# One channel-major step more ahead of the second column group's seven-product steps, in two eighths of a two-layer MLP

## The chip, the cores and the metric

The kernel runs on one core of a Trainium2 chip. The metric is the device time of one execution in microseconds (us). TensorE (PE) multiplies matrices, its weight loads are listed as PEld; VectorE (DVE), ScalarE (ACT) and GpSimd (POOL) work on tiles; SyncE (SP), ACT and POOL issue DMA transfers. Each engine takes its instructions in the order of the program and waits on semaphores for the others.

## What is computed

A decoder trunk of two layers on x of 256 positions by 2048 channels, all in float32. The change lies in the MLP, the second half of each layer:

```
h2 = rms_norm(x, norm2_g[l])
x = x + jnp.square(jax.nn.relu(h2 @ w_up[l])) @ w_down[l]
```

`w_up` is 2048 x 8192 and `w_down` 8192 x 2048. Ahead of the MLP a layer has one input projection, eight attention heads, eight gated channel groups and an output projection; after both layers comes a last norm.

## The kernel before

**Three products for one.** Every float32 weight tile of 128 x 1024 is loaded by SP into `raw` (7 buffers, L155), rounded by ACT into a high part `hi` (6 buffers, L167) and subtracted by DVE into a low part `lo` (6 buffers, L177). The moving operand stands in two parts as well. A product is then three matmuls: high by high (L400), low weight by high (L402), high weight by low (L404).

**The MLP in eighths.** The hidden 8192 channels are worked in eighths of 1024. In the loop over e (L906) pass e makes the hidden eighth e from `w_up` and brings the hidden eighth e-1 through `w_down`. The up product takes 16 *channel-major steps* (`transposed`, L369), called u0 to u15 here: four pairs of 128 channels, four steps each, one weight tile and 24 matmuls a step. Behind every fourth of them `after_up` (L774) takes relu and square, and `to_half` (L638) splits the result in two parts (L640 on ACT, L643 on DVE). In e=7 relu is a DVE operation (L782), in e<7 it is ACT's (L780).

**Seven-product steps.** For `w_down`, 512 columns at a time (a *column group*) can go through `fast` (L407): a two-by-two block product with seven block products in place of eight, in two steps for each group. One such step has four sub-tiles: two loaded ones (`Top`, L179, and `Bottom`, L200) and two sums that DVE makes from them in place (`Sums`, L205, with the four subtractions of L218 to L223). Each sub-tile has a high part on ACT and a low part on DVE; for `Top` they are half as wide (L185, L190). Six products are run in the step (L430, L432, L433), the seventh in the first matmuls of the step behind it (`left_over`, L395). The hidden eighth too must be there in summed form: `sums` (L793) makes four block sums on DVE (L796 to L799), and parts of them are split (L640, L643); the seven-product steps wait for these.

I write F1a and F1b for the first and the second step of the second column group (columns 512 to 1023), F2a and F2b for the third, F0a and F0b for the first.

**The order.** `ORDER` (L63) and `USUAL` (L66) hold for each group the two indices of channel-major steps ahead of which its steps stand, group 0 first. The loop at L919 and L926 merges them into one list:

```
for g, at in enumerate(ORDER.get(e, USUAL)):
...
    quick += zip(at, collect(fast, "w_down", l, (e - 1) * 1024, 512 * g, hidden,
...
for i, one in enumerate(up + down):
    if i in quick:
        steps.append(quick[i])
    steps.append(one)
```

In e=2 to 5 the order is `USUAL`: F1 ahead of u2 and u3, F0 ahead of u7 and u9, F2 ahead of u13 and u14. In e=6 it is F1 at u1 and u2, F2 at u6 and u7, F0 at u11 and u14. In e=7 there are two groups only: F1 at u1 and u2, F0 at u6 and u9.

**How far the other engines work ahead.** The main loop (L999) counts sub-tiles in `done`: a channel-major step is one, a seven-product step four. Ahead of each step it emits high parts up to six sub-tiles ahead and low parts up to five ahead:

```
high_to(done + 2 + ahead)
run_due()
low_to(done + 1 + ahead)
run_due(behind)
load_more()
mm()
```

with `ahead` at 4. `soon(n, fn)` puts work n sub-tiles on (run by `run_due`), `later` puts work into a queue that is worked off at the end of steps, and `behind` holds the second half of a split until one step on.

**Behind a group.** F1 and F2 leave six products in three PSUM banks, the seventh in a fourth. `other_done` (L883) copies the three banks into the staging tile `stage` on ACT (L901), five sub-tiles on the seventh product (L887), and POOL issues four transfers: in the passes before the last of the group they add to an array in DRAM, `far` (L866), and in the last (`FINAL`, L64: e=7 for groups 0 and 1, e=6 for group 2) they add `far` to the staging tile (L897). Nine sub-tiles behind L887 comes `combine` (L808), a chain of seven DVE operations (L814 to L822) that makes the four output blocks; three sub-tiles later ACT scales them (L827), and seven and nine sub-tiles behind combine TensorE transposes them back (L839). F1's third bank is the one that the next pair of channels of the up product uses, so u4 needs it. The staging tile is shared by groups 1 and 2.

Of the kernel before, what the change touches and what calls it, by code (L numbers as in the profile page):

```python
# [59 lines left out]

ORDER = {1: ((7, 10), (13, 14)), 6: ((11, 14), (1, 2), (6, 7)), 7: ((6, 9), (1, 2)), 8: ()}  # L63
FINAL = (7, 7, 6)  # L64
LAST = (4, 6, 8, 10, 0, 2, 12, 14)
USUAL = ((7, 9), (2, 3), (13, 14))  # L66
# [24 lines left out]
def trunk(ctx: ExitStack, tc: tile.TileContext, layout, xT, consts, gains, w, b_sp, w_sp, out):  # L91
# [415 lines left out]
    def layer(l, n1, n2, n3, last):  # L507
# [398 lines left out]
        for e in range(9):  # L906
# [5 lines left out]
            if e:  # L912
                w = 512 * len(ORDER.get(e, USUAL))
                hidden = [hid[e - 1]]
# [3 lines left out]
                               cols=None if e < 8 else [c * P for c in LAST])  # L918
                for g, at in enumerate(ORDER.get(e, USUAL)):  # L919
                    banks = []  # L920
# [147 lines left out]
```

## Time and profile before

| | |
|---|---|
| median of three runs | 2032.21 us (2031.52 to 2033.8) |
| profiled execution | 2032.32 us, of which span 2030.5 us |
| granted TensorE clock | 0.997 of full speed over the span |
| low parts of weights, L177 on DVE | 817 instructions, 1213 ns each, 964.1 us |
| high parts, L167 on ACT | 817 instructions, 1051 ns each, 836.1 us |
| POOL's transfers into `far`, L866 | 92 |

Times in a timeline are microseconds from the span's start: start, busy time, engine, line, operation, the tile written and those read, shapes and count; in brackets stands how long the engine was idle before it and what ended that. Matmuls overlap, so the listed time of one (0.28 us) is longer than the distance to the next. A row with x2 or x3 is two or three instructions in a row, which overlap a little. A row of the waits gives the engine and its line, what it waited for, the sum, the number of times and the longest. The first layer's MLP has its pass e=5 from 712 to 795 us, e=6 from 795 to 880 us and e=7 from 880 us on; in the second layer the same stretches come some 1005 us later.

### The profile page before, as it was taken

How to read it: one execution, taken by the hardware profiler on the slowest of the kernel's cores; microseconds unless marked ns; L12 is line 12 of the kernel's file. 1: busy time of each engine (PE TensorE's matmuls, PEld its weight loads, DVE VectorE, ACT ScalarE, POOL GpSimd, SP SyncE). 2: the span in 40 equal slices, each digit the busy share in tenths (PEclk: the TensorE clock that was granted, in tenths of full speed). 3: DMA queues.
4: the chain of work that ended last, by engine and by line, in shares of the span. 5: the costliest groups of instructions: out<-in, count | busy, mean ns of one | idle time of the engine just before them, and what ended most of it. 6: DMA issues, size and time to landing. Idle time of an engine off the chain costs nothing.

```text
span 2030.5 us, 40718 instructions
## 1 busy us (share of the span) xinstructions
PE 2017.7 (99%) x16834; PEld 1979.0 (97%) x16834; DVE 1577.2 (78%) x1950; ACT 1213.3 (60%) x1613; POOL 157.1 (8%) x200
## 2 busy tenths in 40 slices
PE   9999999999999999999999999999999999999997
PEld 8998999999999999999989989999999999999997
DVE  7566766688888898898856667667888898888985
ACT  7565454566566666765645654556666666667654
POOL 0002300000001000100000032000000000010000
PEclk9999999999999999999999999999999999999998
DMA  9555556567678776865664555565676777777562
GB/s 326 193 168 166 187 187 202 173 229 210 214 221 238 237 227 197 246 220 202 207 213 161 167 187 187 188 199 184 212 227 210 226 234 217 237 215 256 186 217 88
DMA packets 126443, 419.27 MB, mean 206 GB/s; under 512 B 14128, under 2 KB 22064, under 8 KB 126256
## 3 DMA queue, kind: packets, MB, share of 16 engines
q1 hardware_dynamic: 110800, 389.86, 57.3%
q0 software_dynamic: 14304, 23.86, 6.9%
q8 instruction: 132, 2.16, 0.4%
q10 hardware_dynamic: 1152, 2.94, 0.4%
q14 instruction: 55, 0.45, 0.1%
HBM read 394.58 MB, written 22.02 MB: 205 GB/s over the span
## 4 chain that ended last, share of the span: by engine, by line
PE 95%; DVE 3%; ACT 1%; issue 1%; DMA 1%; ACTq 0%; DVEq 0%; SPq 0%
PE acc L402 23%; PE acc L400 23%; PE acc L404 23%; PE acc L461 3%; PE acc L459 3%; PE acc L460 3%; PE aux L430 3%; PE aux L432 3%; PE acc L432 3%; PE aux L433 3%; PE acc L433 3%; PE acc L430 3%; DVE lo L177 1%; ACT hi L167 0%; PE aux L693 0%
## 5 line engine op out<-in xcount | busy, mean ns | idle before, releaser
L167 ACT ACTIVATE hi<-raw 128x1024 fp32r<-128x1024 f32 (+1 forms) x817 | 836.1, 1051 | 495.5 <-DVE raw L219 231.0
L177 DVE TENSOR_TENSOR lo<-raw,hi 128x1024 fp32r<-128x1024 f32 (+1 forms) x817 | 964.1, 1213 | 155.3 <-ACT hi L167 152.0
L400 PE MATMUL acc<-hs,hi 128*128 128x256 f32 x2816 | 781.2, 277 | 0.0
L402 PE MATMUL acc<-hs,lo 128*128 128x256 f32 x2816 | 779.3, 277 | 0.2
L404 PE MATMUL acc<-hs,hi 128*128 128x256 f32 x2816 | 778.2, 276 | 0.0
L402 PEld LDWEIGHTS acc<-hs,lo 128*128 128x128 f32 x2816 | 528.8, 188 | 2.5 <-DVE lo L177 1.8
L400 PEld LDWEIGHTS acc<-hs,hi 128*128 128x128 f32 x2816 | 528.8, 188 | 0.4 <-issue 0.2
L404 PEld LDWEIGHTS acc<-hs,hi 128*128 128x128 f32 x2816 | 528.7, 188 | 0.0
L400 PE MATMUL acc<-half,hi 128*128 128x256 f32 x1344 | 371.9, 277 | 0.0
L402 PE MATMUL acc<-half,lo 128*128 128x256 f32 x1344 | 371.0, 276 | 0.0
L404 PE MATMUL acc<-half,hi 128*128 128x256 f32 x1344 | 371.0, 276 | 0.0
L402 PEld LDWEIGHTS acc<-half,lo 128*128 128x128 f32 x1344 | 252.3, 188 | 0.0
L400 PEld LDWEIGHTS acc<-half,hi 128*128 128x128 f32 x1344 | 252.3, 188 | 0.0
L404 PEld LDWEIGHTS acc<-half,hi 128*128 128x128 f32 x1344 | 252.3, 188 | 0.0
L866 POOL DMA_DIRECT2D far<-ar x92 | 74.7, 983 | 1159.2 <-ACT ar L869 606.3
L432 PE MATMUL acc<-lo,shared 128*128 128x256 f32 x384 | 106.5, 277 | 0.0
L433 PE MATMUL acc<-hi,shared 128*128 128x256 f32 x384 | 106.1, 276 | 0.0
L430 PE MATMUL acc<-hi,shared 128*128 128x256 f32 x384 | 106.0, 276 | 0.0
L459 PE MATMUL acc<-hi,hs 128*128 128x512 f32 x256 | 101.6, 397 | 0.0
L461 PE MATMUL acc<-hi,hs 128*128 128x512 f32 x256 | 100.7, 393 | 0.0
L460 PE MATMUL acc<-lo,hs 128*128 128x512 f32 x256 | 99.9, 390 | 0.5 <-DVE lo L177 0.5
L643 DVE TENSOR_TENSOR half<-ar,half 128x512 fp32r<-128x512 f32 x72 | 49.7, 690 | 62.2 <-ACT half L640 61.2
(163 smaller groups left out, 2560.9 us busy)
## 6 DMA issues: line engine op xcount, KB each, us to landing
raw<-in_w SPq DMA_DIRECT2D x731, 512.0 KB, 4.6
far<-ar POOLq DMA_DIRECT2D x60, 256.0 KB, 6.8
far<-ar POOLq DMA_DIRECT2D x32, 128.0 KB, 4.4
ar<-far POOLq DMA_DIRECT2D x12, 256.0 KB, 9.0
raw<-in_w SPq DMA_DIRECT2D x10, 256.0 KB, 5.2
x<-in_xT SPq DMA_DIRECT2D x7, 256.0 KB, 5.6
out<-x SPq DMA_DIRECT2D x7, 256.0 KB, 3.1
shared<-in_b_sp ACTq DMA_DIRECT2D x2, 512.0 KB, 8.0
```

The costliest lines, as they stand in the source:

```text
L167: act.activation(self.h[:, j * m:(j + 1) * m], self.raw[:, j * m:(j + 1) * m], AF.Copy)
L177: vec.tensor_tensor(lo[:, r], self.raw[:, r], self.h[:, r].bitcast(F32), op=OP.subtract)
L400: pe.matmul(o, lhsT=hi, rhs=xs[:, 0, :], start=(k0 + k == 0 and (two or cb == 0)), stop=False, skip_group_check=True)
L402: pe.matmul(o, lhsT=wt.lo[:, k, cb * P:(cb + 1) * P], rhs=xs[:, 0, :], start=False, stop=False, skip_group_check=True)
L404: pe.matmul(o, lhsT=hi, rhs=xs[:, 1, :], start=False, stop=last, skip_group_check=True)
L430: pe.matmul(o[n], lhsT=xh, rhs=hi, start=(p == 0 and k == 0 and n in fresh), stop=False, skip_group_check=True)
L432: pe.matmul(o[n], lhsT=xh, rhs=lo, start=False, stop=False, skip_group_check=True)
L433: pe.matmul(o[n], lhsT=xl, rhs=hi, start=False, stop=(n in last and p == 1 and k == 1), skip_group_check=True)
L459: pe.matmul(ps, lhsT=xh, rhs=hi, start=(k0 + k == 0), stop=False)
L460: pe.matmul(ps, lhsT=xh, rhs=lo, start=False, stop=False)
L461: pe.matmul(ps, lhsT=xl, rhs=hi, start=False, stop=(k0 + k == KC - 1))
L866: nc.gpsimd.dma_start(far[g][:, r], src, **({} if e == max(g, 1) else {"accum_op": OP.add}))
```

## The change

In e=6 and e=7 the two steps of the second column group stand ahead of u2 and u3, in place of u1 and u2. The other groups stay where they were. As the staged work is counted in sub-tiles, what belongs to F1 moves by one sub-tile with it.

```diff
-ORDER = {1: ((7, 10), (13, 14)), 6: ((11, 14), (1, 2), (6, 7)), 7: ((6, 9), (1, 2)), 8: ()}
+ORDER = {1: ((7, 10), (13, 14)), 6: ((11, 14), (2, 3), (6, 7)), 7: ((6, 9), (2, 3)), 8: ()}
```

The order of the steps in e=6, before and after, to u7:

```
u0 F1a u1 F1b u2 u3 u4 u5 F2a u6 F2b u7
u0 u1 F1a u2 F1b u3 u4 u5 F2a u6 F2b u7
```

and in e=7, to u9:

```
u0 F1a u1 F1b u2 u3 u4 u5 F0a u6 u7 u8 F0b u9
u0 u1 F1a u2 F1b u3 u4 u5 F0a u6 u7 u8 F0b u9
```

## The prediction, made before the result was seen

> **What bounds the kernel now.** I read the page first, for the engine that has no time left, then the waits, for what that engine still waits on, and then the timelines of TensorE (PE), VectorE (DVE) and ScalarE (ACT) around the steps that the diff names.
>
> ```profile
> span 2030.5 us, 40718 instructions
> PE 2017.7 (99%) x16834; PEld 1979.0 (97%) x16834; DVE 1577.2 (78%) x1950; ACT 1213.3 (60%) x1613; POOL 157.1 (8%) x200
> PE 95%; DVE 3%; ACT 1%; issue 1%; DMA 1%; ACTq 0%; DVEq 0%; SPq 0%
> ```
> ```profile
> PEld acc L402 <- DVE lo L177: 1.8, 8, 0.3
> ```
>
> TensorE is busy 99% of the span, yet 3% of the chain runs through DVE: somewhere DVE decides when a matmul starts. The waits name it: eight weight loads of L402 (the product with a weight's low part) waited for the DVE subtraction that makes that part (L177). The timeline of TensorE shows where. I call "first use" of a step its first matmul with a low part: L402 in a channel-major step (u0 to u15 of an eighth), L432 in a seven-product step (F1a and F1b for the two of the second column group, F2a/F2b for the third, F0a/F0b for the first).
>
> ```profile
> 717.72 0.28 PE L432 MATMUL acc<-lo,half 128*128 128x256 f32 x1
> ...
> 729.35 0.28 PE L402 MATMUL acc<-hs,lo 128*128 128x256 f32 x1
> ...
> 732.80 0.28 PE L402 MATMUL acc<-hs,lo 128*128 128x256 f32 x1
> ...
> 735.52 0.28 PE L402 MATMUL acc<-hs,lo 128*128 128x256 f32 x1
> ...
> 738.24 0.28 PE L402 MATMUL acc<-hs,lo 128*128 128x256 f32 x1
> ...
> 798.32 0.28 PE L432 MATMUL acc<-lo,half 128*128 128x256 f32 x1
> ...
> 810.67 0.38 PE L402 MATMUL acc<-hs,lo 128*128 128x256 f32 x1
> ...
> 826.47 0.28 PE L402 MATMUL acc<-hs,lo 128*128 128x256 f32 x1
> ...
> 834.00 0.28 PE L402 MATMUL acc<-hs,lo 128*128 128x256 f32 x1
> ...
> 883.38 0.28 PE L432 MATMUL acc<-lo,half 128*128 128x256 f32 x1
> ...
> 895.72 0.39 PE L402 MATMUL acc<-hs,lo 128*128 128x256 f32 x1
> ...
> 924.38 0.28 PE L400 MATMUL acc<-hs,hi 128*128 128x256 f32 x1
> 924.60 0.39 PE L402 MATMUL acc<-hs,lo 128*128 128x256 f32 x1
> 924.82 0.28 PE L404 MATMUL acc<-hs,hi 128*128 128x256 f32 x1
> ...
> 1803.29 0.28 PE L432 MATMUL acc<-lo,half 128*128 128x256 f32 x1
> ...
> 1815.63 0.38 PE L402 MATMUL acc<-hs,lo 128*128 128x256 f32 x1
> ```
>
> The first five rows are the eighth before (e=5, the plain order, in which F1a and F1b stand ahead of u2 and u3): F1a at 717.72, then u3, u4, u5 and u6 from 729.35 to 738.24. The next four are e=6 (F1a ahead of u1): F1a, u2, u6, u7. Then e=7: F1a, u2, and u9 with its neighbours; last, F1a and u2 of e=6 in the second layer. F1a, a channel-major step, F1b and the start of the next step take 729.35 - 717.72 = 11.63 us in e=5, and the same work takes 12.35 us in e=6, 12.34 in e=7 and 12.34 in the second layer. So some 0.72 us of waiting stands in each changed place. The matmul behind a wait is late as well: 222 ns from L402 to L404 at u9 (924.60 to 924.82) against some 0.12 us elsewhere, so I add 0.1 us behind u2. **Each of the four places holds 0.82 us, 3.3 us in all.** This is what the change can win.
>
> **The change part by part.** It puts one channel-major step (u1) ahead of F1a, in e=6 and e=7 of both layers. No instruction is added or removed; 2 x 2 pairs change place with one channel-major step each.
>
> *The first pair.* DVE reaches F1a behind the sums of the hidden eighth, and in the order of before it is just in time. One step later DVE must also have made one more low part, 1.22 us by the rows below at most, while TensorE has one more step to do, 2.72 us (735.52 - 732.80; a step behind a seven-product step holds its seventh product too and takes 732.80 - 729.35 = 3.45). So the slack grows by about 1.5 us, over the 0.72 us that was short, and e=5 has just this order and no wait in 11.63 us. The 0.82 us go: -0.82.
>
> *The second pair.* Here the row that decides is what DVE waits for between the two pairs.
>
> ```profile
> 731.98 2.36 DVE L177 TENSOR_TENSOR lo<-raw,hi 128x1024 fp32r<-128x1024 f32 x2 [2.75 <-ACT hi L167]
> ...
> 813.10 2.36 DVE L177 TENSOR_TENSOR lo<-raw,hi 128x1024 fp32r<-128x1024 f32 x2 [1.35 <-ACT hi L167]
> ...
> 821.82 0.69 DVE L643 TENSOR_TENSOR half<-ar,half 128x512 fp32r<-128x512 f32 x1 [0.70 <-ACT half L640]
> 822.77 2.36 DVE L177 TENSOR_TENSOR lo<-raw,hi 128x1024 fp32r<-128x1024 f32 x2 [0.26 <-ACT hi L167]
> ...
> 829.57 3.64 DVE L177 TENSOR_TENSOR lo<-raw,hi 128x1024 fp32r<-128x1024 f32 x3
> ...
> 836.64 2.36 DVE L177 TENSOR_TENSOR lo<-raw,hi 128x1024 fp32r<-128x1024 f32 x2 [2.30 <-ACT hi L167]
> ```
> ```profile
> 729.43 1.58 ACT L901 ACTIVATE ar<-acc 128x512 f32<-128x512 f32 x3 [1.83 <-PE acc L433]
> 730.88 2.02 ACT L167 ACTIVATE hi<-raw 128x1024 fp32r<-128x1024 f32 x2
> ...
> 810.54 1.58 ACT L901 ACTIVATE ar<-acc 128x512 f32<-128x512 f32 x3 [0.42 <-PE acc L433]
> 811.99 2.02 ACT L167 ACTIVATE hi<-raw 128x1024 fp32r<-128x1024 f32 x2
> ```
>
> When F1b ends, ACT copies its three banks (L901), and what stands behind the copies in ACT's order has to wait: the high parts (L167) of the next weights, and with them DVE's low parts. DVE then stands idle until the first of them is there: 1.35 us in e=6, 2.75 us in e=5, where F1b comes a step later. In e=5 the part that DVE waits for is u5's; u4's was made ahead of the copies. It begins 731.98 - 729.35 = 2.63 us after u3's first use. In e=6 of before u4's begins at 813.10 and u5's one part later, at 814.24 (half of a 2.36 us pair, with overlap).
>
> After the change, by e=5's rows: F1a at 798.32 + 2.72 = 801.04, u3 at 801.04 + 11.63 = 812.67, u5's low part at 812.67 + 2.63 = 815.30. **That is 1.06 us later than before, although TensorE is 0.82 us earlier.** The slack ahead of F2a falls by some 1.9 us.
>
> From there DVE works without a pause longer than 0.7 us. u6's part ends at 822.77 + 2.36 = 825.13 for a first use at 826.47 (1.34 us of slack), u7's at 829.57 + 3.64 = 833.21 for 834.00 (0.79 us). Moved by 1.06, u7's would end at 834.27. One thing gives a little back: F1b's last copy (L887, 0.26 us of ACT's time ahead of the high part of F2a's last weights) also moves one step on, behind that high part, and the 0.26 us wait above goes with it, less what the copy then costs u6's high part. I take 0.87 instead of 1.06, 834.08, and with the 0.05 us from the end of a low part to its matmul 834.13 against 834.00: +0.1, or +0.3 without the gift. I take **+0.2 us for e=6**, bounds -0.8 (no delay of DVE at all) and +0.4. Behind F2b DVE waits for ACT's copies again, 2.30 us, and starts anew from TensorE's time, so no more than this is carried on.
>
> In e=7 the pair behind is F0a ahead of u6 and F0b ahead of u9:
>
> ```profile
> 898.14 2.36 DVE L177 TENSOR_TENSOR lo<-raw,hi 128x1024 fp32r<-128x1024 f32 x2 [1.34 <-ACT hi L167]
> ...
> 918.15 0.68 DVE L782 SCALAR_TENSOR_TENSOR ar<-acc,nR 128x512 f32<-128x512 f32 x1
> 918.75 0.41 DVE L814 TENSOR_TENSOR ar<-ar 128x256 f32<-128x256 f32 x1
> ...
> 921.25 0.42 DVE L822 TENSOR_TENSOR ar<-ar 128x256 f32<-128x256 f32 x1
> 921.59 1.22 DVE L177 TENSOR_TENSOR lo<-raw,hi 128x1024 fp32r<-128x1024 f32 x1
> 922.72 0.68 DVE L643 TENSOR_TENSOR half<-ar,half 128x512 fp32r<-128x512 f32 x1
> 923.33 8.03 DVE L177 TENSOR_TENSOR lo<-raw,hi 128x1024 fp32r<-128x1024 f32 x7
> ```
> ```profile
> 919.53 0.63 ACT L640 ACTIVATE half<-ar 128x512 fp32r<-128x512 f32 x1
> ```
>
> The same sum: u3 at 883.38 + 2.72 + 11.63 = 897.73, u5's part at 900.36 against 899.28, 1.08 us later. Here nothing takes it up: u9's part (the first of the last group) ends at 923.33 + 1.22 = 924.55, and its matmul stands at 924.60, so u9 waits for DVE already. All DVE work up to u9's part is the same, combine (L814 to L822) included. Its place changes: one step later it stands behind the low part of 921.59 and L643, not ahead of them. L643 needs ACT's L640, done at 919.53 + 0.63 = 920.16; moved by 1.08 that is 921.24, while DVE would be there at 920.97. So 0.27 us more: u9 at 924.60 + 1.08 + 0.27, **+1.4 us for e=7**, bounds +0.3 (half of the delay lost on the way and no such gap) and +1.7.
>
> *The rest.* What F1 does behind its last step moves one step with it and no further: the copies, the four transfers that POOL issues, and in e=7 combine, its scaling and its transposes. The up-bank that F1b holds has one step of 3.45 us until u4 needs it, against copies of 1.58 us for all three, as in e=5, which shows no wait there: 0. The loads on SP keep their number and size and the order of e=5: 0. The last quarter's transfer comes latest:
>
> ```profile
> 819.61 0.36 ACT L887 ACTIVATE ar<-aux 128x256 f32<-128x256 f32 x1
> ```
> ```profile
> DMA to landing us min/median/max: 6.8/8.7/12.0
> ```
>
> Its copy moves from 819.61 with the pair (1.06 us) and behind three operations for u3's result (0.63 us each, by L640) and a high part (1.01, half of 2.02), to 823.6 by that estimate, and ACT overwrites the staging tile when F2b ends, near 834.1. The four transfers of this stretch landed within 6.8 to 12.0 us: by the median the tile is free near 832.7, by the longest near 836.0, 1.9 us late, and ACT's high parts would stand behind it. I take 0, and a chance of 3 in 100 for more, which rival 3 holds. The Trainium skill ("DMA: Bandwidth & Descriptors", section on the anatomy of one DMA on the gpsimd path) gives about 2.0 us and the bytes over 436 GB/s; by that estimate 128 KB would land in 2.3 us and this chance would be none. The trace's 6.8 us at the least speaks against it for these accumulating transfers.
>
> **Sum:** 2 x (0.2 + 1.4) = +3.2 us, in which the 0.82 us won at each first pair is counted already, since both ends are measured against the first use of before. The profiled execution took 2032.32 us (the span and 1.8 us around it), 0.1 above the median of the three runs: 2032.3 + 3.2 = **2035.5 us**.
>
> **The rivals.**
> 1. *The waits go and nothing is late next.* 4 x 0.82 = 3.3 us less: 2029.0. For it: e=5 has no wait at all. Against it: e=5 has four channel-major steps from F1b to the next pair, e=6 and e=7 would have three, and u9 has no slack. The Trainium skill ("Perfetto Trace Analysis", section Optimization Strategy) says to find the gaps of the most-contended engine and have what they wait for ready sooner; by that rule this is the case to expect. The trace agrees that the gaps are DVE's; the rows of the second pair say that they move. Chance 0.07.
> 2. *They cancel.* DVE starts u5's part up to 0.8 us sooner than in e=5, since ACT has less in front of it; then e=6 gains and e=7 loses about as much: 2032.3 within 1.3. Chance 0.18.
> 3. *Slower by more than can be missed.* Both second pairs of both layers hang on the start of u5's part, so each 0.1 us that it comes later than 2.63 us after u3 costs 0.4 us. From 0.22 us on (another copy, or ACT's relu and square ahead of F2a's last high part) it passes 4.1 us; at 0.4 us later it gives 2035.5 + 1.6 = 2037.1. For it: e=7's hidden part needs DVE's L782 in that very place. Against it: the copies and the two high parts behind them take 1.58 and 2.02 us in e=5 and in e=6 alike. Chance 0.25.
>
> **How the numbers follow.** The forecast has 0.50, the rivals 0.07, 0.18 and 0.25. A measurement of this kernel can tell about 0.2%, 4.1 us, from no change. The forecast and rivals 1 and 2 lie within that: 0.75, of which I give 0.02 to faster for a first-pair gain that also takes u9's wait with it. Same 0.73, slower 0.25. The range runs from 2031.0 (rival 2 at its lower end; what it leaves out is rival 1 and little more) to 2037.4 (most of rival 3).
>
> **What would show it.** Right: F1a to u3 in 11.63 us in e=6 and e=7; DVE's wait for ACT behind F1b at 2.7 us instead of 1.35; L402 waiting for L177 at u6 and u7 of e=6 and at u6 and u9 of e=7; combine behind F0b's last low part. Wrong: L402 with no wait left at all (rival 1), a wait at u9 of 0.1 us as before (rival 2), waits at F2a or F0a themselves, at u4's bank, or ACT's L901 waiting for a transfer. The first pair still waiting would refute the first step.

## The result, and the profile after

The changed kernel took 2036.07 us in the median of 15 runs (2034.44 to 2039.13), the kernel before 2031.77 us (2031.32 to 2033.8, 15 runs). The ratio is 1.0021, with a 95% interval of 1.0014 to 1.0027: about 4 us slower. From lowest run to lowest run it is 3.1 us, and between the two profiled executions 2035.07 - 2032.32 = 2.75 us.

The first lines of the page after, and its waits of TensorE on DVE's low parts:

```profile
span 2033.3 us, 40716 instructions
PE 2016.4 (99%) x16834; PEld 1977.8 (97%) x16834; DVE 1578.1 (78%) x1950; ACT 1215.1 (60%) x1613; POOL 157.0 (8%) x200
```
```profile
PEld acc L402 <- DVE lo L177: 5.4, 8, 1.5
PE acc L402 <- DVE lo L177: 3.7, 6, 1.3
```

The instructions of each engine are the same in number, the busy times differ by under 2 us on every engine, and the share of TensorE is still 99%. What is new is the waits of weight loads for the low part: again eight, but 5.4 us in place of 1.8, the longest 1.5 us. The timeline of TensorE says where they are now (start, busy time, engine, line; the bracket is idle time and what ended it):

```profile
801.00 0.28 PE L432 MATMUL acc<-lo,half 128*128 128x256 f32 x1
...
812.63 0.28 PE L402 MATMUL acc<-hs,lo 128*128 128x256 f32 x1
...
826.04 0.39 PE L402 MATMUL acc<-hs,lo 128*128 128x256 f32 x1 [0.26 <-DVE lo L177]
...
834.11 0.38 PE L402 MATMUL acc<-hs,lo 128*128 128x256 f32 x1
...
886.30 0.28 PE L432 MATMUL acc<-lo,half 128*128 128x256 f32 x1
...
897.93 0.28 PE L402 MATMUL acc<-hs,lo 128*128 128x256 f32 x1
...
910.11 0.28 PE L430 MATMUL aux<-hi,shared 128*128 128x256 f32 x1
910.51 0.39 PE L432 MATMUL aux<-lo,shared 128*128 128x256 f32 x1
...
911.73 0.38 PE L402 MATMUL acc<-hs,lo 128*128 128x256 f32 x1 [0.24 <-DVE lo L177]
...
924.69 0.28 PE L400 MATMUL acc<-hs,hi 128*128 128x256 f32 x1
926.30 0.39 PE L402 MATMUL acc<-hs,lo 128*128 128x256 f32 x1 [1.33 <-DVE lo L177]
...
1932.82 0.39 PE L402 MATMUL acc<-hs,lo 128*128 128x256 f32 x1 [1.33 <-DVE lo L177]
```

F1a to u3 takes 812.63 - 801.00 = 11.63 us in e=6 and 897.93 - 886.30 = 11.63 us in e=7: the waits of the first pair are gone. But u6 (826.04) and u7 (834.11) of e=6 now wait, and so do F0a's last product (910.51), u6 (911.73) and u9 (926.30) of e=7. At u7 the run is 0.11 us behind the kernel before (834.00), at u9 1.70 us (924.60), and at u9 of the second layer 3.26 us, by this row of the kernel before:

```profile
1929.56 0.38 PE L402 MATMUL acc<-hs,lo 128*128 128x256 f32 x1
```

On DVE and ACT between the pairs, after:

```profile
815.27 1.23 DVE L177 TENSOR_TENSOR lo<-raw,hi 128x1024 fp32r<-128x1024 f32 x1 [2.75 <-ACT hi L167]
...
900.57 1.23 DVE L177 TENSOR_TENSOR lo<-raw,hi 128x1024 fp32r<-128x1024 f32 x1 [2.77 <-ACT hi L167]
...
920.11 1.22 DVE L177 TENSOR_TENSOR lo<-raw,hi 128x1024 fp32r<-128x1024 f32 x1
921.57 0.69 DVE L643 TENSOR_TENSOR half<-ar,half 128x512 fp32r<-128x512 f32 x1 [0.24 <-ACT half L640]
922.18 0.42 DVE L814 TENSOR_TENSOR ar<-ar 128x256 f32<-128x256 f32 x1
...
925.02 2.35 DVE L177 TENSOR_TENSOR lo<-raw,hi 128x1024 fp32r<-128x1024 f32 x2
```
```profile
812.71 1.58 ACT L901 ACTIVATE ar<-acc 128x512 f32<-128x512 f32 x3 [1.83 <-PE acc L433]
814.16 1.07 ACT L167 ACTIVATE hi<-raw 128x1024 fp32r<-128x1024 f32 x1
...
823.41 0.36 ACT L887 ACTIVATE ar<-aux 128x256 f32<-128x256 f32 x1
```

ACT waits for the end of F1b, copies three banks (1.58 us), and only then makes u5's high part; DVE stands idle for 2.75 us until that is there, where it was 1.35 us before. In e=7 the low part of F0b's last weights (920.11), L643 and combine (from 922.18) run without a pause but for 0.24 us, and u9's low part starts at 925.02 and ends 0.06 us ahead of its matmul.

### The profile page after: what moved, and what is told of

It is laid out like the page before. It is cut to its first block, busy times and chain, and to the rows that moved or that the text cites. A ratio compares the mean times of both kernels' runs of the same rounds, so it can differ in the third digit from the quotient of the medians.

```text
span 2033.3 us, 40716 instructions
## 1 busy us (share of the span) xinstructions
PE 2016.4 (99%) x16834; PEld 1977.8 (97%) x16834; DVE 1578.1 (78%) x1950; ACT 1215.1 (60%) x1613; POOL 157.0 (8%) x200
## 4 chain that ended last, share of the span: by engine, by line
PE 95%; DVE 2%; ACT 1%; issue 1%; DMA 1%; ACTq 0%; DVEq 0%; SPq 0%
PE acc L402 23%; PE acc L400 22%; PE acc L404 22%; PE acc L432 3%; PE acc L433 3%; PE acc L430 3%; PE acc L461 3%; PE acc L459 3%; PE acc L460 3%; PE aux L430 2%; PE aux L433 2%; PE aux L432 2%; DVE lo L177 1%; ACT hi L167 1%; PE aux L693 0%
## 5 line engine op out<-in xcount | busy, mean ns | idle before, releaser
L402 PE MATMUL acc<-hs,lo 128*128 128x256 f32 x2816 | 779.0, 277 | 3.7 <-DVE lo L177 3.7
L400 PE MATMUL acc<-hs,hi 128*128 128x256 f32 x2816 | 781.2, 277 | 0.0
L404 PE MATMUL acc<-hs,hi 128*128 128x256 f32 x2816 | 778.2, 276 | 0.0
L402 PEld LDWEIGHTS acc<-hs,lo 128*128 128x128 f32 x2816 | 528.8, 188 | 5.7 <-DVE lo L177 5.4
L400 PEld LDWEIGHTS acc<-hs,hi 128*128 128x128 f32 x2816 | 528.7, 188 | 0.4 <-issue 0.2
L404 PEld LDWEIGHTS acc<-hs,hi 128*128 128x128 f32 x2816 | 528.6, 188 | 0.0
L400 PE MATMUL acc<-half,hi 128*128 128x256 f32 x1344 | 371.9, 277 | 0.0
L404 PE MATMUL acc<-half,hi 128*128 128x256 f32 x1344 | 371.0, 276 | 0.0
L402 PE MATMUL acc<-half,lo 128*128 128x256 f32 x1344 | 371.0, 276 | 0.0
L402 PEld LDWEIGHTS acc<-half,lo 128*128 128x128 f32 x1344 | 252.3, 188 | 0.0
L400 PEld LDWEIGHTS acc<-half,hi 128*128 128x128 f32 x1344 | 252.3, 188 | 0.0
L404 PEld LDWEIGHTS acc<-half,hi 128*128 128x128 f32 x1344 | 252.3, 188 | 0.0
L432 PE MATMUL acc<-lo,shared 128*128 128x256 f32 x384 | 106.2, 277 | 0.0
L643 DVE TENSOR_TENSOR half<-ar,half 128x512 fp32r<-128x512 f32 x72 | 49.8, 691 | 62.5 <-ACT half L640 61.4
```

What stands on the lines that cost most here:

```text
L400: pe.matmul(o, lhsT=hi, rhs=xs[:, 0, :], start=(k0 + k == 0 and (two or cb == 0)), stop=False, skip_group_check=True)
L402: pe.matmul(o, lhsT=wt.lo[:, k, cb * P:(cb + 1) * P], rhs=xs[:, 0, :], start=False, stop=False, skip_group_check=True)
L404: pe.matmul(o, lhsT=hi, rhs=xs[:, 1, :], start=False, stop=last, skip_group_check=True)
L432: pe.matmul(o[n], lhsT=xh, rhs=lo, start=False, stop=False, skip_group_check=True)
```

## The experiments

Theory A is the prediction's: one step later the first pair no longer waits, but the copies behind F1b hold up ACT's high parts and so DVE, which is then late for the second pair. Rival B puts the loss on what F1 does behind its last step: its staging transfers or combine's new place. The kernels below were timed beside the kernel before, whose medians were 2031.96 us for the first four, 2031.76 us for the next four and 2032.04 us for the last two.

**Each eighth alone.** First e=6 only, then e=7 only:

```diff
-... 6: ((11, 14), (2, 3), (6, 7)), 7: ((6, 9), (2, 3)), 8: ()}
+... 6: ((11, 14), (2, 3), (6, 7)), 7: ((6, 9), (1, 2)), 8: ()}
```

> Only e=6 is changed, e=7 keeps the order of before. Theory A (the waits of the first pair go, and DVE, held by the copies behind F1b, is late for the second pair): in each layer u7 of e=6 comes 0.1 to 0.2 us later than before, so the whole run is 0.2 to 0.4 us longer than before. Rival B (the loss comes from what F1 does behind its last step: staging transfers, combine): e=6 has the transfers but no combine of F1, so it shows half of the loss or more, +1.5 to +2 us, if the transfers are the cause, and a gain of 1.6 us (2 x 0.82) if combine alone is.

```diff
-... 6: ((11, 14), (2, 3), (6, 7)), 7: ((6, 9), (2, 3)), 8: ()}
+... 6: ((11, 14), (1, 2), (6, 7)), 7: ((6, 9), (2, 3)), 8: ()}
```

> Only e=7 is changed. Theory A: u9 of e=7 comes 1.4 to 1.5 us later in each layer, +2.8 to +3.0 us against before in the profiled execution, nearly all of the change's loss. Rival B with transfers as the cause: about half of the loss. Rival B with combine as the cause: the whole loss and the gain of e=6 less, +4.5 us.

Measured: e=6 alone 2032.36 us, 0.4 us above before (ratio 1.0003, 0.9994 to 1.0012); e=7 alone 2034.97 us, 3.0 us above (1.0015, 1.0007 to 1.0024). Both are A's numbers, and B's are missed in both. The intervals by themselves leave room for B's numbers (up to 2.4 us for e=6, 1.4 to 4.9 us for e=7), but the profiles don't. With e=6 alone it takes 833.60 - 800.51 = 33.09 us from F1a to u7, 0.13 us more than the kernel before less one step (834.00 - 798.32 - 2.72 = 32.96); with e=7 alone it takes 926.29 - 886.31 = 39.98 us from F1a to u9, 1.48 us more than before less one step (924.60 - 883.38 - 2.72 = 38.50). The wait at u9 is there in full with e=7 alone:

```profile
924.69 0.28 PE L400 MATMUL acc<-hs,hi 128*128 128x256 f32 x1
926.29 0.39 PE L402 MATMUL acc<-hs,lo 128*128 128x256 f32 x1 [1.32 <-DVE lo L177]
```

**The copies doubled.**

```diff
-                for i in (2, 0, 1):
+                for i in (2, 0, 1) * (2 if e > 5 and g == 1 else 1):
```

> The change, with F1's three bank copies made twice in e=6 and e=7 (the second time the same values into the same places), which adds 1.5 us of ACT's time behind F1b. Theory A: DVE's wait for ACT behind F1b grows from 2.75 to 4.2 us and everything up to u7 of e=6 and u9 of e=7 moves by 1.5 us: 2 x 2 x 1.5 = 6 us longer than the change, about 9 us longer than before. Rival B: the copies have idle time around them (ACT waits 3 us for DVE soon after); 0 to 0.5 us longer than the change.

Measured: 2041.06 us (2040.63 to 2041.42, 5 runs), 9.1 us above before (ratio 1.0045, 1.0031 to 1.0059), and 5.7 to 6.1 us above the changed kernel (by the medians, with 2035.37 us for it from the next run, and by the profiled executions, 2041.21 against 2035.07). Its ACT, DVE and TensorE:

```profile
812.62 3.05 ACT L901 ACTIVATE ar<-acc 128x512 f32<-128x512 f32 x6 [1.83 <-PE acc L433]
```
```profile
816.64 1.23 DVE L177 TENSOR_TENSOR lo<-raw,hi 128x1024 fp32r<-128x1024 f32 x1 [4.21 <-ACT hi L167]
```
```profile
835.45 0.38 PE L402 MATMUL acc<-hs,lo 128*128 128x256 f32 x1
...
929.09 0.39 PE L402 MATMUL acc<-hs,lo 128*128 128x256 f32 x1 [1.33 <-DVE lo L177]
```

The copies grow by 3.05 - 1.58 = 1.47 us, DVE's wait by 4.21 - 2.75 = 1.46 us, u7 of e=6 comes 835.45 - 834.11 = 1.34 us later and u9 of e=7 929.09 - 926.30 = 2.79 us. What ACT does there arrives at TensorE almost in full, four times a run.

**The changed kernel again**, unaltered:

> The changed kernel once more, unaltered, for a second profile and more times. Theory A: the profiled execution shows the same waits at u6 and u7 of e=6 and at F0a's last product, u6 and u9 of e=7, and 3 us more than before. If the scatter of the changed kernel (2034.4 to 2039.1 us in 15 runs, wider than before's) comes from waits that come and go, a slower profile shows another wait: a transfer ahead of combine, or ACT's copies waiting for a staging transfer.

Measured: 2035.37 us (2034.98 to 2037.48, 11 runs), 3.4 us above before (1.0020, 1.0011 to 1.0028). Its profile shows the same waits at the same places (u9 waits 1.6 us from L400 to L402). To see where the scatter comes from, it was profiled twice more at the end, with a guess from these profiles (theory C: the distance between matmuls, which stays longer for a while behind some waits, makes it):

> The changed kernel unaltered, for a third profile. In some profiles the distance between matmul starts stays at 118 ns instead of 113 ns for 8 to 44 us behind a wait of TensorE, at a granted clock of 1.00. Theory C: such stretches begin only at waits and make the upward scatter; then a run above 2035.1 us shows stretches whose length times 0.04 is about what it is longer, and none begins away from a wait or a step of another kind. If they have nothing to do with waits, they begin in plain steps as well.

> The changed kernel unaltered, for a fourth profile, with the same question: does a longer execution hold longer stretches at 118 ns between matmuls, each beginning at a wait of TensorE (theory C), or is its extra time elsewhere (outside the span, at the start of the run, or in longer waits)?

Measured: 2035.07 and 2035.62 us; the kernel before, run once beside them, took 2034.04 us. Neither holds a stretch of more than 4 us at 118 ns in e=6 or e=7, and in the second the 0.6 us more were there before the first channel-major step (its first L400 stands at 52.43 us, in the other three at 51.8 to 51.9). None of the four was an execution of over 2036 us, so for this kernel C is neither shown nor refuted. A case for it stands in a kernel further below, the one with F0b later: its profiled execution keeps the longer distance for some 21 us in each layer (see the last section), and its span is 1.7 us above the median span of its runs (2031.9 against 2030.2 us).

**The copies spread.** Only the bank that u4 needs is copied at once; the two others stand ahead of the next sums' high part, where ACT waits for DVE anyway.

```diff
-                for i in (2, 0, 1):
-                    act.activation(stage[:, 512 * i:512 * (i + 1)], banks[i], AF.Copy)
+                def copy(i):
+                    act.activation(stage[:, 512 * i:512 * (i + 1)], banks[i], AF.Copy)
+                split = e > 5 and g == 1
+                for i in (2,) if split else (2, 0, 1):
+                    copy(i)
+                if split:
+                    waiting.append(lambda: (copy(0), copy(1)))
...
             if not subs[n_high[0]].loads:
                 low_to(n_high[0] - subs[n_high[0]].second)
+                while waiting:
+                    waiting.pop()()
```

> The change, with two of F1's three bank copies in e=6 and e=7 put off until ACT waits for the next sums anyway (just ahead of the high part of F2a's or F0a's first sum); the third, whose bank u4 needs, stays. Theory A: u5's low part starts 1.0 us sooner (1.65 instead of 2.63 us behind u3's first use), e=6 loses its waits at u6 and u7 (0.86 us faster than before per layer), u9 of e=7 stays 0.5 us later than before; together 0.7 us faster than before, 3.9 us faster than the change. Rival B (transfers or combine): the transfers start later, so no gain over the change, or a loss.

Measured: 2031.41 us, 0.35 us below before (ratio 1.0000, 0.9991 to 1.0009), where A had 0.7; the changed kernel was 3.4 and 4.3 us above. The waits at u6 and u7 of e=6 are gone and u9's is left (1.5 us in each layer), as A had it. ACT and DVE:

```profile
812.90 0.60 ACT L901 ACTIVATE ar<-acc 128x512 f32<-128x512 f32 x1 [1.83 <-PE acc L433]
...
815.82 1.07 ACT L901 ACTIVATE ar<-acc 128x512 f32<-128x512 f32 x2
818.89 1.06 ACT L167 ACTIVATE hi<-raw 128x1024 fp32r<-128x1024 f32 x1 [2.00 <-DVE raw L219]
```
```profile
814.48 1.22 DVE L177 TENSOR_TENSOR lo<-raw,hi 128x1024 fp32r<-128x1024 f32 x1 [1.77 <-ACT hi L167]
```

DVE's wait falls from 2.75 to 1.77 us, and the two later copies cost nothing, since ACT still waits 2.00 us behind them. POOL issues the first three transfers from 816.70 us on here, in place of 814.09 us, and the loss is gone all the same, so B in its form with transfers falls.

**Combine earlier, and later.** One sub-tile earlier, which is its place on DVE before the change:

```diff
-                    soon(9, lambda: combine(stage, 4 * g, here))
+                    soon(9 - (e == 7), lambda: combine(stage, 4 * g, here))
```

> The change, with F1's combine in e=7 one sub-tile sooner, where it stood on DVE before the change. Theory A: only the 0.25 us go in which DVE waits for ACT ahead of L643, 0.3 to 0.5 us faster than the change, still 2.7 us or more slower than before. Rival B (combine's new place makes the loss): back to the time of before or better.

and four later, behind u9's low part:

```diff
-                    soon(9, lambda: combine(stage, 4 * g, here))
+                    soon(9 + 4 * (e == 7), lambda: combine(stage, 4 * g, here, late=e == 7))
...
-            wait = 6 if o else 7
+            wait = 6 if o else 5 if late else 7
```

> The change, with F1's combine in e=7 four sub-tiles later, behind u9's low part (its transposes two sub-tiles closer to it). Theory A: u9's wait of 1.5 us goes, the waits at F0a and u6 stay: 1.6 us per layer, 3.2 us faster than the change, within 0.5 us of before. If DVE's lateness is then felt at u10 (0.8 us of slack by the sum), some of it is given back.

Measured: earlier 2034.98 us, 3.2 us above before (1.0016, 1.0007 to 1.0024), u9 at 925.86 in its profile; later 2032.25 us, 0.5 us above before (1.0003, 0.9994 to 1.0012), with u9's low part ahead of combine and no wait at u9:

```profile
922.74 1.23 DVE L177 TENSOR_TENSOR lo<-raw,hi 128x1024 fp32r<-128x1024 f32 x1 [0.26 <-ACT hi L167]
923.88 0.42 DVE L814 TENSOR_TENSOR ar<-ar 128x256 f32<-128x256 f32 x1
```
```profile
924.92 0.28 PE L400 MATMUL acc<-hs,hi 128*128 128x256 f32 x1
925.04 0.28 PE L402 MATMUL acc<-hs,lo 128*128 128x256 f32 x1
```

So combine's new place is not the cause (the old one gives back some tenths), but its 2.8 us of DVE ahead of u9's low part is what leaves u9 without slack.

**Both mends together**, the spread copies and the later combine:

> Both: two copies put off, and combine behind u9's low part. Theory A: no wait of TensorE is left in e=6 and e=7 of either layer; 3.5 us faster than before (2 x (0.86 + 0.91)), near 2028.4 us. If the cause is elsewhere: no faster than before.

Measured: 2028.91 us (2027.8 to 2029.91), 2.85 us below the kernel before, where A had 3.5, and below the changed one as well (ratio to before 0.9985, 0.9976 to 0.9993). No wait of an L402 or L432 matmul for DVE is left; u9 of e=7 follows its L400 by 0.12 us:

```profile
922.61 0.28 PE L400 MATMUL acc<-hs,hi 128*128 128x256 f32 x1
922.73 0.28 PE L402 MATMUL acc<-hs,lo 128*128 128x256 f32 x1
```

**The first group's steps moved too.** First F0a one step later in e=7, which gives the four steps between the pairs that e=5 has; then F0b alone one step later:

```diff
-... 7: ((6, 9), (2, 3)), 8: ()}
+... 7: ((7, 9), (2, 3)), 8: ()}
```

> The change, with the first step of e=7's first group one channel-major step later as well (ahead of u7 instead of u6), so that four steps lie between F1b and F0a, as in e=5. Theory A: the waits at F0a and behind it go (0.9 us with the reloads), but DVE has the same work up to u9 and starts it at the same time, so u9's wait grows by the same 0.9 us: within 0.5 us of the change. Rival 1 of the prediction (four steps between the pairs are enough): e=7 shows no wait, 3 us faster than the change.

```diff
-... 7: ((6, 9), (2, 3)), 8: ()}
+... 7: ((6, 10), (2, 3)), 8: ()}
```

> The change, with the second step of e=7's first group one channel-major step later (ahead of u10 instead of u9). Theory A: one step of 2.7 us on TensorE against one low part of 1.1 us on DVE more ahead of the low part that came late: the wait behind F0b shrinks by 1.5 us to about 0.1 us, 2.5 to 3 us faster than the change, within 0.7 us of before. If combine's place behind F0b's last low part makes the loss by itself, nothing changes.

Measured: with F0a later 2034.80 us, 2.8 us above before (1.0011, 1.0002 to 1.0020); the waits at F0a and behind it are gone, and u9 still waits, 1.75 us from L400 to L402 against 1.61:

```profile
925.06 0.28 PE L400 MATMUL acc<-hs,hi 128*128 128x256 f32 x1
926.81 0.38 PE L402 MATMUL acc<-hs,lo 128*128 128x256 f32 x1 [1.48 <-DVE lo L177]
```

By the distances to the kernel before that is 0.6 to 1.5 us better than the changed kernel, where A expected at most 0.5 (the two were not timed side by side). In this profile u9 stands later all the same, 926.81 against 926.30, because TensorE ran slower for a stretch ahead of e=7 (see the last section). From the start of u5's low part to the end of u9's DVE takes 926.76 - 901.85 = 24.91 us here and 25.67 us in the changed kernel: its pauses for ACT ahead of F0a's last part (0.23 and 0.26 us) are gone too, which A had counted as work that stays. But the four steps of e=5 do not bring e=5's freedom from waits. With F0b later 2032.69 us, 0.65 us above before (1.0000, 0.9991 to 1.0009), without a wait at u9 or behind F0b; its waits of L402 loads come to 2.3 us in six, at u6 and u7 of e=6 and at u6 of e=7. The prediction held the short distance between the pairs against its rival 1, and the expectation above tested that distance as the cause. By itself it does not decide: with F0a later the waits at F0a and u6 go, and the one at u9 stays. These runs fit the account that what counts is how much DVE has to do, from u5's low part on, until a low part that is due.

## Why the prediction was right

*The first pair.* The forecast was 11.63 us from F1a to u3, and it was 11.63 us in both eighths.

*The start of u5's low part.* 2.63 us behind u3's first use, by the row of e=5; measured 815.27 - 812.63 = 2.64 us in e=6 and 900.57 - 897.93 = 2.64 us in e=7. That a place with the same order of steps stood in the trace of before made this term safe. Doubling and spreading the copies moved it by +1.5 and -1.0 us, so the copies are shown to set when DVE goes on, nearly microsecond for microsecond.

*The second pair of e=6.* Forecast u7 at 834.13, measured 834.11; the net of both layers, 2 x 0.2 us, was 0.4 us with e=6 alone. The 0.19 us that the sum took off for the moved copy (L887) came in size (18.79 us from the start of u5's part to the end of u7's, against 18.97 before), but not where the prediction saw it:

```profile
822.59 0.69 DVE L643 TENSOR_TENSOR half<-ar,half 128x512 fp32r<-128x512 f32 x1 [0.44 <-ACT half L640]
823.54 2.45 DVE L177 TENSOR_TENSOR lo<-raw,hi 128x1024 fp32r<-128x1024 f32 x2 [0.26 <-ACT hi L167]
```

The wait of 0.26 us ahead of the low parts, which was to go, is still there. The wait ahead of L643 fell instead, from 0.70 to 0.44 us, because the copy no longer stands ahead of the relu and square that lead to it. This step came out right in part by luck.

*The second pair of e=7.* Forecast 1.35 us behind before, which with 0.13 from e=6 is 926.08; measured 926.30. The gap ahead of L643 was 0.24 us for 0.27. From the start of u5's part to the end of u9's it took 926.24 - 900.57 = 25.67 us against 25.27 before (924.55 - 899.28), so 0.40 us more and not 0.27: the term was 0.13 us short. The rows account for it. From the start of F0b's last low part to L643 it is 921.57 - 920.11 = 1.46 us, against 922.72 - 921.59 = 1.13 us before, so that gap costs 0.33 us, as the overlap of two instructions in a row goes with it. The other 0.07 us or so lies in the four low parts from F0a's last one on, first before, then after:

```profile
907.94 4.63 DVE L177 TENSOR_TENSOR lo<-raw,hi 128x1024 fp32r<-128x1024 f32 x4 [0.26 <-ACT hi L167]
```
```profile
909.23 4.71 DVE L177 TENSOR_TENSOR lo<-raw,hi 128x1024 fp32r<-128x1024 f32 x4 [0.26 <-ACT hi L167]
```

The copy L887 stands between their high parts now (909.10 on ACT); before, ACT waited for DVE right behind it. The prediction gave this copy no term in e=7.

*What was off.* The list of signs held waits at F0a itself to be against the forecast; there was one (910.11 to 910.51, some 0.28 us over the usual distance). The same lateness reached F0a's last product first, by the sum's own rows (u6's part follows the last low part of F0a directly), and it did not change when u9 came. The landing of the staging transfers was put at 6.8 us and more; after the change the last quarter of e=6 landed in 3.8 us and all four within 8.8 us, early enough for the staging tile either way. Those 3.8 us are still longer than the prediction's estimate of 2.3 us for 128 KB from the Trainium skill ("DMA: Bandwidth & Descriptors", section on the anatomy of one DMA on the gpsimd path).

*The size.* The sum was 3.2 us. At u9 of the second layer the change is 3.26 us behind, the lowest runs differ by 3.1 us and the second set of runs by 3.4 us; the first set's median difference is 4.3 us. The changed kernel's times spread more upward (to 2039.13) than those of before, and part of that lies outside the span: 1.7 to 2.9 us, against 1.7 to 1.9 us for the kernel before in the second set. The median span of the changed kernel was 2033.5 us in the first set and 2033.6 us in the second; that of the kernel before was 2030.1 us in the second, so inside the span the loss is 3.4 to 3.5 us. Its four profiled executions took 2035.07 to 2035.62 us, in the lower half of the first set, so what makes the longest spans (to 2037.0 us) stays open. The kernel before had one of 2033.2 us as well, timed beside the last two kernels. By its size the first set comes near rival 3, but that would have needed u5's low part to come later than it did.

That 3.26 us came so near the sum is partly luck: u9 of the first layer was 1.70 us behind for a forecast of 1.48, and at F1a of the second layer it was 1807.53 - 1803.29 - 2.72 = 1.52 us.

*The rule.* The Trainium skill ("Perfetto Trace Analysis", section Optimization Strategy) has one look for the gaps of the most-contended engine and make what they wait for ready sooner. The trace agrees on where the gaps were, but by itself the rule gave rival 1 and 2029.0 us. That time came only with the two mends (2028.91 us), which also remove the next gaps.

## What to carry to other kernels

When a wait is taken from the busiest engine by moving work, follow the engine that was late to the next place where it is due: here DVE had the same work until u9, and what counted was when it could start. An engine that copies results out and also prepares the next operands, in one order, can pass its wait for a result on to those operands, as ACT does here; copies that nobody needs yet belong where that engine is idle anyway. If the same order of steps occurs elsewhere in the trace, its rows are a good forecast of the new place, here to 0.01 us.

## What the hardware showed

TensorE has two paces with no wait between matmuls and the same granted clock. Usually a channel-major step runs at 113 to 114 ns from start to start; behind some waits it stays at 118 ns for a while, as in the kernel with F0a later from u7 of e=6 on. Here is the same stretch in that kernel and then in the kernel before (stretch, its length, busy time and number of matmuls, and so on; after the engines the granted clock, the share of DMA time and GB/s):

```profile
834.00:878.00 44.00, 43.97 (x375) 43.94 (x375) 38.12 (x47) 32.67 (x45) 4.45 (x5) 1.00 0.79 255
```
```profile
834.00:878.00 44.00, 44.00 (x389) 44.00 (x388) 38.48 (x49) 31.07 (x42) 4.45 (x5) 1.00 0.77 250
```

375 matmuls in place of 389 make 14 x 0.113 = 1.6 us in this stretch. The changed kernel, with the same wait at 834 us, starts 386 in it. In the four profiles of the changed kernel it came once for long, from the wait at u6 of e=7 in the second layer on (1918 to 1942 us). The kernel with F0b later held it in both layers, from the same wait on:

```profile
911.87:933.13 21.26, 21.26 (x181) 21.26 (x181) 20.79 (x26) 14.97 (x19) 0.00 (x0) 1.00 0.66 229
```

At 0.113 us 188 matmuls would start in these 21.26 us, so it costs 0.8 us in each layer. In e=6 and e=7 of all the profiles, every such stretch of over 4 us sets in behind a weight load that waited for DVE, and the kernel with both mends, which has no such wait, has no such stretch. Most of these waits are not followed by one, though. What sets the pace, and when it goes back, no run here tells.

A matmul behind a late weight load is followed by a longer distance as well: 222 ns from L402 to L404 at u9 before the change, against 0.12 us without a wait, so such a wait costs 0.1 us more than its own length. Two ACT copies of 128x512 placed in idle time cost nothing that shows (the 1.07 us of the spread copies), while the same two ahead of a high part cost 1.0 us at TensorE: from F1a of e=6 to F1a of e=7 the changed kernel takes 886.30 - 801.00 = 85.30 us, and the one with the copies spread 885.51 - 801.19 = 84.32 us.
